# Two-stage SSD chunks and pinned gathered rows in a hybrid decoder layer

## The chip, the cores and the metric

The kernel runs on one core of one Trainium2 chip. The metric is device time in microseconds (us). The engines are named as the profile names them: PE is TensorE (matmul), PEld its weight load, DVE is VectorE, ACT is ScalarE, POOL is GpSimd and SP is SyncE, which only issues DMAs here.

## The reference

One decoder layer works on 16 meta tokens and 512 tokens of width 1024, in float32. Cut to what matters:

```python
u = rmsnorm(h, norm_mix_w)
z, xbc, dt_raw, conf_in = split(u @ w_in)
y_ssd  = ssd_mixer(z, xbc, dt_raw, ...)       # 16 heads in 4 groups, chunks of 128 tokens
y_conf = conformer_conv(conf_in, ...)         # GLU, depthwise conv of width 31, LayerNorm, silu
h = h + concat([y_ssd, y_conf]) @ w_out
h = h + peer_ffn(rmsnorm(h, norm_ffn_w), ...) # 8 heads x 16 of 128*128 single-neuron experts
out = rmsnorm(h, norm_final_w)[:, 16:]

# ssd, per group g and chunk c:
y  = (C B^T * exp(segsum(dt*a))) @ (dt*x) + exp(cumsum) * (C @ state)
state = state * exp(sum) + B^T @ (decay * dt * x)

# peer_ffn, per token: scores on two key halves, top 16 of each, top 16 of the sums, softmax gate
y = sum over the 128 chosen experts e of gelu(x . w_down[e]) * gate[e] * w_up[e]
```

## The kernel before, in words

The program is straight-line code. Tile, a scheduler at build time, orders the instructions of every engine by a priority, which is the order in which they are written, shifted by `early(n)` (as if written n instructions sooner) and `late(n)`, and by when a simulated timeline takes their inputs as ready. At run time each engine works through its own queue in that order and waits on semaphores.

*Mixer.* Nineteen weight blocks of the input projection are taken in the order of `ORDER`: `z` blocks (gate of the SSD), `x` blocks (x, B and C, with a convolution of width 4 and transposes through PE), and `c` blocks (conformer, with a convolution of 30 multiply-adds on DVE, L422, marked `late`). As soon as its inputs are there, `ssd(g)` is written for group g = 0 to 3, with `early(SSDP)`, so ahead of the convolutions. It goes through five chunks: chunk 0 holds the 16 meta tokens and makes only a state. Chunks 1 to 4 take PSUM tiles of one bank each: `pa` for B·C (L532) and C·state (L533), `pe` for the mask and the cumulated decay (L536, L539), from which ACT makes four exponentials (L545), and `pd` for the chunk's output product (L551) and its state product (L560). DVE multiplies the exponentials with B·C (L546), forms y from C·state (L548), the skip term (L549), the output product (L552) and the gate (L553), and carries the state on (L564, L565). The root mean square goes through ACT (L554) and POOL (L259), and y is stored to a DRAM buffer yD for groups 0 to 2. Tiles without a tag share four PSUM banks ("pb"): those of the SSD, of the transposes of the x blocks (L352, L355) and of the LayerNorm sums. The projections have four more ("pa").

*Output projection.* `out_part([0])` and `out_part([1])` use the SSD's half of the output, `out_part([2, 3])` the conformer's. Between them stand the LayerNorm sums (L657), the rows made of them on PE (L402) and the normalisation of eight blocks (L672 to L677). Weights are split into a high and a low part, the low one by an accumulating DMA from POOL's queue (L186).

*PEER.* Tokens 0 to 383 are computed densely over all experts: `down(i)` makes the activations of 128 experts, `up_prep(i)` and `up_mm(i)` gate them and multiply with w_up. Tokens 384 to 511 are computed sparsely: 128 rows of w_down and then of w_up, in four alternating batches of 32, are gathered by indirect DMAs (L895, on POOL), and DVE takes a dot product (L911) or an accumulation (L918) for each, 256 rows in all. `pump(x)` writes x of these rows, fractions carried over. The selection of experts (`second(t)`, for t = 3, 0, 1, 2) comes first. Then `gate_map` writes, for each of 12 blocks of 32 tokens, four quarters: one-hot maps on DVE (L946, L947, L949), products on PE (L954, L955) and copies on ACT (L957). 86 `down` blocks stand behind the gate maps in the text and are marked `early(AHP)`, so they are worked on at the same time. The main loop then goes over 128 expert blocks.

During the gate maps the gathered rows go through two buffers (`gat1`), in the main loop through six (`gat2`). `keep_in_program_order(r)` gives an instruction one added edge: in its engine's queue it stands behind the instruction that was written last before it on that engine. Gathers have it always, the row operations only when `paced` is filled, which before the change happens ahead of the main loop.

Of the kernel before, what the change touches and what calls it, by code (L numbers as in the profile page):

```python
# [15 lines left out]
AF = mybir.ActivationFunctionType  # L16
OP = mybir.AluOpType
# [18 lines left out]
LNP = 500  # L36
AHP = 1000
SPL = 0
SPRATE = (4.0, 1.03, 3.33, 0)
NQ = 2  # L40
NT = 4
HOLD = 2
# [75 lines left out]
def body(ctx, tc, I, out):  # L118
    nc = tc.nc
    V, S, G, E = nc.vector, nc.scalar, nc.gpsimd, nc.tensor  # L120
# [7 lines left out]
    def ps(tag="pb"):  # L128
        return psp.tile([128, 512], F32, name=tag, tag=tag)
# [4 lines left out]
    def late(n):  # L134
        return tc.high_priority(offset=-n)

    def mem(a, n):
        assert a + n <= SLAB
        return M[:, a:a + n]
# [13 lines left out]
    def load(dst, src):  # L153
        return nc.sync.dma_start(dst, src)
# [4 lines left out]
    def mm3(o, lh, ll, rh, rl, first, last):  # L159
        E.matmul(o, lh, rh, start=first, stop=False)  # L160
        E.matmul(o, lh, rl, start=False, stop=False)  # L161
        E.matmul(o, ll, rh, start=False, stop=last)  # L162
# [85 lines left out]
    def stat(n):  # L248
        a = stp[0] % 128
        if a + n > 128:  # L250
            a = 0
        stp[0] = a + n
        return st[:, a:a + n]

    def rstd_of(ss, n, scale, parts=128):
        v = stat(n)[:parts]
        V.tensor_scalar(v, ss, scale, EPS, op0=OP.mult, op1=OP.add)  # L257
        r = stat(n)[:parts]
        G.tensor_tensor(r, v, neghalf[:parts, :n], op=OP.pow)  # L259
        return r  # L260
# [31 lines left out]
    for n, t in enumerate(MO):  # L292
# [6 lines left out]
        r = rstd_of(ss, 1, 1.0 / D, parts)  # L299
        for half in range(2):  # L300
            hs = slice(512 * half, 512 * half + 512)
# [41 lines left out]
    Bt = mem(B0, 2048).rearrange("p (c n) -> p c n", c=4)  # L343
    BT = mem(BT0, 2112).rearrange("p (g t) -> p g t", g=4)
    CT = mem(CT0, 2048).rearrange("p (g t) -> p g t", g=4)
# [162 lines left out]
    h4 = lambda a: a.rearrange("p (h d) -> p h d", h=4)  # L508
    rot = [0]

    def ssd(g):
        dtv, nacs, eacs, cdB, wst, a3 = [DTV[k] for k in ("dtv", "nacs", "eacs", "cdB", "wst", "a3")]
        state = states[g % 2]
        ss = stat(4)
        ysl = []
        for c in range(5):
            np_ = NM if c == 0 else 128
            hs = slice(16 * c + 4 * g, 16 * c + 4 * g + 4)
            hb = lambda a: a[:np_, hs, None].to_broadcast([np_, 4, 64])
            n = rot[0]  # L520
            rot[0] += 1
            xc = XS[g % 2][:np_, c, :]
            xdt, xw = xdts[n % 3], xws[n % 3]
            V.tensor_tensor(h4(xdt[:np_]), h4(xc), hb(dtv), op=OP.mult)
            if c < 4:
                V.tensor_tensor(h4(xw[:np_]), h4(xdt[:np_]), hb(wst), op=OP.mult)
            pd = ps()
            if c > 0:
                t0 = 128 * (c - 1)
                V.tensor_tensor(h4(xc), h4(xc), rowb[:, 32 + 4 * g:36 + 4 * g, None].to_broadcast([128, 4, 64]), op=OP.mult)  # L530
                pa = ps()
                E.matmul(pa[:, 0:128], BT[:, g, NM + t0:NM + t0 + 128], CT[:, g, t0:t0 + 128], start=True, stop=True)  # L532
                E.matmul(pa[:, 128:384], CT[:, g, t0:t0 + 128], state, start=True, stop=True)  # L533
                pe = ps()
                pe4 = pe.rearrange("p (r l) -> p r l", r=4)
                E.matmul(pe4, identb, mnegb[:, None, :].to_broadcast([128, 4, 128]), start=True, stop=False)  # L536
                for r in range(4):
                    q = 16 * ((c - 1) % 2) + 4 * g + r
                    E.matmul(pe4[:, r, :], sel[:96, q:q + 1].to_broadcast([96, 128]),  # L539
                             a3[:96, 128 * ((c - 1) // 2):128 * ((c - 1) // 2) + 128],  # L540
                             start=False, stop=r == 3)
                em = EM[n % 3].rearrange("p (r l) -> p r l", r=4)
                for r in range(4):
                    h = 16 * c + 4 * g + r
                    S.activation(em[:, r, :], pe4[:, r, :], AF.Exp, bias=nacs[:, h:h + 1])  # L545
                V.tensor_tensor(em, em, pa[:, None, 0:128].to_broadcast([128, 4, 128]), op=OP.mult)  # L546
                y_ = ybs[n % 3] if g < 3 else YL[c - 1]
                V.tensor_tensor(h4(y_), h4(pa[:, 128:384]), hb(eacs), op=OP.mult)  # L548
                V.tensor_tensor(y_, y_, xc, op=OP.add)  # L549
                for r in range(4):  # L550
                    E.matmul(pd[:, 64 * r:64 * r + 64], em[:, r, :], xdt[:, 64 * r:64 * r + 64], start=True, stop=True)  # L551
                V.tensor_tensor(y_, y_, pd[:, 0:256], op=OP.add)  # L552
                V.scalar_tensor_tensor(y_, y_, 0.5, ZB[g % 2][:, c - 1, :], op0=OP.mult, op1=OP.mult)  # L553
                S.activation(xdt, y_, AF.Square, accum_out=ss[:, c - 1:c])  # L554
                rs = rstd_of(ss[:, c - 1:c], 1, 1.0 / 256)
                S.activation(y_, y_, AF.Copy, scale=rs)
                if g < 3:
                    load(yD[c - 1, :, 256 * g:256 * g + 256], y_)
            if c < 4:
                E.matmul(pd[:, 256:512], Bt[:np_, c, 128 * g:128 * g + 128], xw[:np_], start=True, stop=True)  # L560
                if c == 0:
                    S.activation(state, pd[:, 256:512], AF.Copy)
                else:
                    V.tensor_tensor(h4(state), h4(state), hb(cdB), op=OP.mult)  # L564
                    V.tensor_tensor(state, state, pd[:, 256:512], op=OP.add)  # L565


    done = set()
# [1 line left out]
    for o in ORDER:  # L570
        {"z": z_block, "x": x_block, "c": c_block}[o[0]](int(o[1]))
        if o == "z0":
            dt_chain()
        done.add(o)
        while left and {"x4", "x5", "x6", "x7", "x%d" % left[0], "z%d" % left[0]} <= done:
            with early(SSDP):
                ssd(left.pop(0))
# [104 lines left out]
    for t in range(4):  # L682
# [3 lines left out]
        for hf in range(2):  # L686
            hs = slice(512 * hf, 512 * hf + 512)
# [3 lines left out]
        r = rstd_of(ss, 1, 1.0 / D)  # L691
        for hf in range(2):
            hs = slice(512 * hf, 512 * hf + 512)
# [97 lines left out]
    for h in range(8):  # L791
        wh, wl = split_n(raw_n(I["wq"][h].rearrange("p c n -> p (c n)"), 2048), 2048, V)
        for f in range(2):
# [7 lines left out]
            for t in range(4):  # L801
                E.matmul(psc[:, 128 * t:128 * t + 128], qT[:, 128 * t:128 * t + 128], keys[:, 2 * h + f, :],
                         start=True, stop=True)
# [97 lines left out]
    paced = []  # L901
# [22 lines left out]
    def pump(x):  # L924
        spn[0] += x
        while spn[0] >= 1:
            spn[0] -= 1
            next(sp, None)

    for t in (3, 0, 1, 2):  # L930
        second(t)
        if t < 3:
            pump(SPRATE[3])

# [3 lines left out]
    def gate_map(n, b):  # L938
        gb = GBUF[n % 2]
        half = lambda a: a.rearrange("p t (j s) -> p t j s", s=2)  # L940
        io = iota16.rearrange("p (j s) -> p j s", s=2)[:, None].to_broadcast([128, TB, 64, 2])
        for q in range(GB // TB):
            t0 = GB * b + TB * q
            ob, oa = OB[q % 2], OA[q % 2]
            col = lambda a: a[:, t0:t0 + TB, None, :].to_broadcast([128, TB, 64, 2])
            V.tensor_tensor(half(ob), io, col(i2d), op=OP.is_equal)  # L946
            V.tensor_tensor(half(OE), io, col(i1d), op=OP.is_equal)  # L947
            for s in range(2):
                V.tensor_tensor(half(oa[s]), half(OE), col(gd[s]), op=OP.mult)  # L949
            for k0 in range(0, TB, 4):  # L950
                p = ps()
                for k in range(4):
                    po = p[:, 128 * k:128 * k + 128]
                    E.matmul(po, ob[:, k0 + k, :], oa[0][:, k0 + k, :], start=True, stop=False)  # L954
                    E.matmul(po, ob[:, k0 + k, :], oa[1][:, k0 + k, :], start=False, stop=True)  # L955
                c = TB * q + k0
                S.activation(gb.rearrange("p i t -> p t i")[:, c:c + 4, :], p.rearrange("p (t i) -> p t i", t=4),  # L957
                             AF.Copy, scale=1.0 / GS)
        for q in range(4 if n < NB - 2 else 0):
            load(GD[b, :, 32 * q:32 * q + 32, :], gb[:, 32 * q:32 * q + 32, :])  # L960

# [23 lines left out]
    def up_mm(i, Y, ops, ms, hfs=(0, 1)):  # L985
        sh, sl, wh, wl = ops
        f, l = i == 0, i == 127
        for m in ms:
            c = slice(128 * m, 128 * m + 128)
            for hf in hfs:  # L990
                d = slice(512 * hf, 512 * hf + 512)
                mm3(Y[m][hf], sh[:, c], sl[:, c], wh[:, d], wl[:, d], f, l)

    for n in range(NB):
        gate_map(n, n if n < NB - 2 else 2 * NB - 3 - n)
        with late(SPL):
            pump(SPRATE[0])

    with early(AHP):
        for i in range(NQ, NAHEAD):  # L1000
# [1 line left out]

    ring[0] = gat2
    gn[0] = 0
    paced.append(True)
    ops = {}
    Y = [[ps("pa"), ps("pa")], [ps("pa"), ps("pa")], [ps(), ps()]]
    for i in range(128):
        for j in {127 - NT: range(128 - NT, 128)}.get(i, () if i > 127 - NT else (i + 1,)):
            if NAHEAD <= j < 128:  # L1010
                down(j, "pb", False, V)
        pump(0 if i < HOLD else SPRATE[1] if i < NAHEAD else SPRATE[2])
        ops[i] = up_prep(i, V)
# [48 lines left out]
```

## Time and profile before

| | |
|---|---|
| median of 3 runs | 1705.93 us (1703.87 to 1708.15) |
| the profiled execution's own time | 1709.63 us |
| span in its profile | 1707.9 us |
| mean granted PE clock | 0.973 |
| DMA | 425.38 MB, mean 249 GB/s |

The span runs from the first to the last instruction; the time has some 2 us around it. The profile's page gives the busy time of each engine and, in 40 slices of 42.7 us, where it falls. Other views group instructions by line, list who waited for whom, list instructions in order of time, or sum up chosen stretches. In the timeline a row holds the start, the time, the engine, the line, the operation with output and inputs, and in brackets the idle time before it with what ended it. In a row of waits, "A <- B: 6.3, 4, 2.2" means that A waited for B 6.3 us in total, in 4 times, 2.2 us at the longest.

### The profile page before, as it was taken

What the parts mean: (1) busy time and instruction counts of PE and PEld (TensorE: products, weight loads), DVE (VectorE), ACT (ScalarE), POOL (GpSimd) and SP (SyncE); (2) the same over time, 40 slices, a digit from 0 to 9 for tenths busy, and PEclk for the clock granted to TensorE, in tenths of its full rate; (3) what the DMA queues carried; (4) which work ended last, traced back from release to release, by engine and by line L of the source; (5) the groups of instructions that cost most, each with busy time, mean ns of one, the idle gap of its engine ahead of it and who ended that gap; (6) DMA issues with size and microseconds to landing.
All of it is one profiled execution on the core that took longest, in us unless ns stands there. A gap on an engine that the chain in (4) does not pass through costs nothing. (4 is left out here: it accounts for less than half of the span.)

```text
span 1707.9 us, 26157 instructions
## 1 busy us (share of the span) xinstructions
PE 1643.6 (96%) x9529; PEld 1487.2 (87%) x9529; DVE 1397.6 (82%) x2864; ACT 770.7 (45%) x1155; POOL 397.6 (23%) x336
## 2 busy tenths in 40 slices
PE   7999999799899999899999999999999999999997
PEld 7999999577788999898889988888888899999996
DVE  4998999974469998989889458888888889888885
ACT  5566554445333344356668533333333333333333
POOL 1111110110000003233410013222222254454540
PEclk9999999589999999999999999999999999999999
DMA  6877574454422458799888679999999899999892
GB/s 209 194 176 164 143 163 123 141 136 119 128 83 75 131 177 271 271 301 327 306 308 301 211 233 364 347 348 357 352 341 355 317 341 363 357 347 348 324 328 86
DMA packets 165185, 425.38 MB, mean 249 GB/s; under 512 B 14384, under 2 KB 81200, under 8 KB 159424
## 3 DMA queue, kind: packets, MB, share of 16 engines
q1 hardware_dynamic: 121568, 261.17, 43.8%
q0 software_dynamic: 43488, 162.55, 31.4%
q8 instruction: 74, 1.21, 0.3%
q14 instruction: 55, 0.45, 0.1%
HBM read 381.72 MB, written 41.94 MB: 248 GB/s over the span
## 5 line engine op out<-in xcount | busy, mean ns | idle before, releaser
L161 PE MATMUL pa<-MR 128*128 128x512 f32 (+3 forms) x2120 | 731.3, 345 | 3.4 <-DMA MR<-wout 3.4
L160 PE MATMUL pa<-MR 128*128 128x512 f32 (+3 forms) x2120 | 728.5, 345 | 6.1 <-ACT M L777 1.7
L162 PE MATMUL pa<-MR 128*128 128x512 f32 (+3 forms) x2120 | 693.8, 345 | 6.5 <-DVE MR L755 5.1
L160 PEld LDWEIGHTS pa<-MR 128*128 128x128 f32 x2120 | 405.2, 191 | 38.6 <-ACT M L777 2.3
L162 PEld LDWEIGHTS pa<-MR 128*128 128x128 f32 x2120 | 404.0, 191 | 38.3 <-DVE MR L755 5.4
L161 PEld LDWEIGHTS pa<-MR 128*128 128x128 f32 x2120 | 404.9, 191 | 34.9 <-DMA MR<-wout 4.6
L754 ACT ACTIVATE MR<-M 128x1024 fp32r<-128x1024 f32 (+1 forms) x264 | 285.8, 1083 | 307.1 <-PE pa L161 130.4
L755 DVE TENSOR_TENSOR MR<-M,MR 128x1024 fp32r<-128x1024 f32 (+1 forms) x264 | 330.0, 1251 | 97.4 <-ACT MR L754 96.5
L895 POOL DMA_INDIRECT M<-wu,M x128 | 177.7, 1388 | 387.4 <-DVE M L918 255.6
L895 POOL DMA_INDIRECT M<-wd,M x128 | 156.2, 1220 | 471.8 <-DVE M L911 209.6
L161 PE MATMUL pb<-MR 128*128 128x384 f32 (+1 forms) x576 | 206.6, 359 | 0.0
L160 PE MATMUL pb<-MR 128*128 128x384 f32 (+1 forms) x576 | 206.6, 359 | 0.0
L162 PE MATMUL pb<-MR 128*128 128x384 f32 (+1 forms) x576 | 205.0, 359 | 0.0
L981 ACT ACTIVATE MR<-M 128x384 fp32r<-128x384 f32 x128 | 67.0, 523 | 262.2 <-issue 202.9
L918 DVE SCALAR_TENSOR_TENSOR M<-M 128x1024 f32<-128x1024 f32 x128 | 163.5, 1278 | 15.4 <-DMA M<-wu,M 15.1
L422 DVE SCALAR_TENSOR_TENSOR M<-M 128x512 f32<-128x512 f32 x240 | 173.6, 743 | 2.6 <-ACT M L420 1.5
L911 DVE SCALAR_TENSOR_TENSOR M<-M 128x1024 f32<-128x1024 f32 x128 | 154.6, 1218 | 14.0 <-DMA M<-wd,M 13.7
L160 PEld LDWEIGHTS pb<-MR 128*128 128x128 f32 x576 | 108.1, 188 | 11.3
L161 PEld LDWEIGHTS pb<-MR 128*128 128x128 f32 x576 | 108.1, 188 | 11.2
L982 DVE TENSOR_TENSOR MR<-M,MR 128x384 fp32r<-128x384 f32 x128 | 71.0, 555 | 56.6 <-ACT MR L981 56.6
L162 PEld LDWEIGHTS pb<-MR 128*128 128x128 f32 x576 | 108.1, 188 | 10.4
L957 ACT ACTIVATE M<-pb 128x512 f32<-128x512 f32 x96 | 97.3, 1151 | 36.8 <-PE pb L955 35.2
(221 smaller groups left out, 1485.4 us busy)
## 6 DMA issues: line engine op xcount, KB each, us to landing
M<-wdT SPq DMA_DIRECT2D x128, 512.0 KB, 5.1
M<-wu SPq DMA_DIRECT2D x128, 512.0 KB, 6.5
GD<-M SPq DMA_DIRECT2D x40, 512.0 KB, 6.3
M<-GD SPq DMA_DIRECT2D x32, 640.0 KB, 7.6
M<-win SPq DMA_DIRECT2D x19, 1024.0 KB, 5.5
MR<-win POOLq DMA_DIRECT2D x38, 512.0 KB, 6.7
HD<-M SPq DMA_DIRECT2D x88, 192.0 KB, 4.3
M<-HD SPq DMA_DIRECT2D x88, 192.0 KB, 6.2
```

Source lines behind the costliest of these rows:

```text
L160: E.matmul(o, lh, rh, start=first, stop=False)
L161: E.matmul(o, lh, rl, start=False, stop=False)
L162: E.matmul(o, ll, rh, start=False, stop=last)
L422: V.scalar_tensor_tensor(o, gl[:, j:j + 512], cw[:, j:j + 1], o, op0=OP.mult, op1=OP.add)
L754: S.activation(wh, raw, AF.Copy)
L755: leng.tensor_tensor(wl, raw, wh.bitcast(F32), op=OP.subtract)
L895: r = G.indirect_dma_start(out=g, out_offset=None, in_=src, in_offset=bass.IndirectOffsetOnAxis(ap=e3[:, k:k + 1], axis=0))
L911: use(V.scalar_tensor_tensor(g, g, 1.0, x2s, op0=OP.mult, op1=OP.mult, accum_out=dots[:, k:k + 1]))
L918: use(V.scalar_tensor_tensor(h1[3], g, act3[:, k:k + 1], h1[3], op0=OP.mult, op1=OP.add))
L957: S.activation(gb.rearrange("p i t -> p t i")[:, c:c + 4, :], p.rearrange("p (t i) -> p t i", t=4), AF.Copy, scale=1.0 / GS)
L981: S.activation(sh, sf, AF.Copy)
L982: V.tensor_tensor(sl, sf, sh.bitcast(F32), op=OP.subtract)
```

## The change

`ssd(g)` is written in two stages. `prepare(c)` holds all of a chunk that needs no state: the scaled inputs, B·C, the mask and the cumulated decay, the exponentials and their product with B·C. `finish(c)` holds C·state, the output and state products, the update of the state, and y. They are written as prepare(0), then for each c prepare(c+1) and finish(c). The output and state products go into the bank of the exponentials, so a chunk takes two banks instead of three; chunk 0 takes one for itself in `finish`. In `finish` the state is updated ahead of y.

The gathered rows are distributed anew. `SPRATE` holds, before and after: per gate map 4.0 (after all four quarters) and 3.0 (0.75 after each quarter); per main-loop block up to 87, 1.03 and 1.0; from 88 on, 3.33 and 3.3; after each of three selections 0 and 2; and, new, 6 after the last gate map. `paced` is filled ahead of the gate maps instead of ahead of the main loop, so each row operation there gets the added edge too.

```diff
-SPRATE = (4.0, 1.03, 3.33, 0)
+SPRATE = (3.0, 1.0, 3.3, 2, 6)
...
-        for c in range(5):
+        ready = {}
+
+        def heads(c, np_=128):
+            hs = slice(16 * c + 4 * g, 16 * c + 4 * g + 4)
+            return lambda a: a[:np_, hs, None].to_broadcast([np_, 4, 64])
+
+        def prepare(c):
             np_ = NM if c == 0 else 128
...
-            pd = ps()
+            em = pa = pe = None
             if c > 0:
...
                 pa = ps()
                 E.matmul(pa[:, 0:128], BT[:, g, NM + t0:NM + t0 + 128], CT[:, g, t0:t0 + 128], start=True, stop=True)
-                E.matmul(pa[:, 128:384], CT[:, g, t0:t0 + 128], state, start=True, stop=True)
                 pe = ps()
...
                 V.tensor_tensor(em, em, pa[:, None, 0:128].to_broadcast([128, 4, 128]), op=OP.mult)
+            ready[c] = n, np_, xc, xdt, xw, em, pa, pe
+
+        def finish(c):
+            n, np_, xc, xdt, xw, em, pa, pd = ready.pop(c)
+            hb = heads(c)
+            if c == 0:
+                pd = ps()
+            else:
+                t0 = 128 * (c - 1)
+                E.matmul(pa[:, 128:384], CT[:, g, t0:t0 + 128], state, start=True, stop=True)
+                for r in range(4):
+                    E.matmul(pd[:, 64 * r:64 * r + 64], em[:, r, :], xdt[:, 64 * r:64 * r + 64], start=True, stop=True)
+            if c < 4:
+                E.matmul(pd[:, 256:512], Bt[:np_, c, 128 * g:128 * g + 128], xw[:np_], start=True, stop=True)
+                if c == 0:
+                    S.activation(state, pd[:, 256:512], AF.Copy)
+                else:
+                    V.tensor_tensor(h4(state), h4(state), hb(cdB), op=OP.mult)
+                    V.tensor_tensor(state, state, pd[:, 256:512], op=OP.add)
+            if c > 0:
                 y_ = ybs[n % 3] if g < 3 else YL[c - 1]
...
+        prepare(0)
+        for c in range(5):
             if c < 4:
-                E.matmul(pd[:, 256:512], Bt[:np_, c, 128 * g:128 * g + 128], xw[:np_], start=True, stop=True)
...
+                prepare(c + 1)
+            finish(c)
...
+            pump(SPRATE[0] / 4)
...
+    paced.append(True)
     for n in range(NB):
         gate_map(n, n if n < NB - 2 else 2 * NB - 3 - n)
-        with late(SPL):
-            pump(SPRATE[0])
+    pump(SPRATE[4])
...
-    paced.append(True)
```

More of the change, by code (lines that the diff above doesn't have):

```diff
@@ L514, in ssd @@
         ss = stat(4)
-        ysl = []
-        for c in range(5):
+        ready = {}
[3 more added lines that the diff above has]
+        def prepare(c):
             np_ = NM if c == 0 else 128
-            hs = slice(16 * c + 4 * g, 16 * c + 4 * g + 4)
-            hb = lambda a: a[:np_, hs, None].to_broadcast([np_, 4, 64])
+            hb = heads(c, np_)
             n = rot[0]
@@ L549, in ssd @@
                 V.tensor_tensor(y_, y_, xc, op=OP.add)
-                for r in range(4):
-                    E.matmul(pd[:, 64 * r:64 * r + 64], em[:, r, :], xdt[:, 64 * r:64 * r + 64], start=True, stop=True)
                 V.tensor_tensor(y_, y_, pd[:, 0:256], op=OP.add)
@@ L558, in ssd @@
                     load(yD[c - 1, :, 256 * g:256 * g + 256], y_)
+        prepare(0)
+        for c in range(5):
             if c < 4:
-                E.matmul(pd[:, 256:512], Bt[:np_, c, 128 * g:128 * g + 128], xw[:np_], start=True, stop=True)
[L561 to L565, printed above, removed]
+                prepare(c + 1)
+            finish(c)
     done = set()
```

## The prediction

> **What bounds the kernel now.** I read the page of the profile first, then the table of stretches, then the waits of each engine in the two places where TensorE is not full, then the timeline there. The page says that TensorE (PE) is the engine to feed, and where it starves.
>
> ```profile
> span 1707.9 us, 26157 instructions
> PE 1643.6 (96%) x9529; PEld 1487.2 (87%) x9529; DVE 1397.6 (82%) x2864; ACT 770.7 (45%) x1155; POOL 397.6 (23%) x336
> ...
> PE   7999999799899999899999999999999999999997
> ...
> DVE  4998999974469998989889458888888889888885
> ...
> PEclk9999999589999999999999999999999999999999
> ```
>
> A slice is 42.7 us. PE has a hole in slice 8 (from 299 us), with a granted clock near half, and small ones in slices 11 and 17; VectorE (DVE) is full at the first hole. The next table puts stretches side by side; its columns are length, then PE, weight load, DVE, ACT and POOL busy time, granted clock, share of the DMA engines and GB/s.
>
> ```profile
> 300.00:340.00 40.00, 28.27 (x99) 20.83 (x100) 39.85 (x89) 16.80 (x47) 5.56 (x5) 0.53 0.49 147
> 360.00:386.60 26.60, 23.74 (x114) 20.02 (x113) 12.96 (x40) 13.29 (x31) 3.01 (x4) 0.74 0.45 119
> 386.60:408.00 21.40, 18.91 (x87) 15.21 (x85) 18.77 (x31) 15.77 (x20) 0.91 (x1) 0.98 0.41 99
> 680.00:700.00 20.00, 14.57 (x72) 13.93 (x71) 20.00 (x67) 3.85 (x6) 3.50 (x4) 0.83 0.67 218
> 820.00:840.00 20.00, 17.48 (x127) 16.06 (x127) 14.63 (x20) 9.89 (x12) 7.51 (x3) 0.91 0.90 311
> 950.00:1018.00 68.00, 66.60 (x378) 63.95 (x377) 24.41 (x30) 26.88 (x38) 5.07 (x5) 1.00 0.69 225
> 1020.00:1680.00 660.00, 660.00 (x3128) 573.97 (x3127) 560.57 (x835) 240.22 (x329) 244.49 (x201) 1.00 0.94 340
> ...
> 600.00:1018.00 418.00, 401.66 (x2754) 385.65 (x2753) 341.73 (x680) 226.93 (x286) 90.02 (x56) 0.99 0.79 271
> ```
>
> From 1020 to 1680 us PE is busy in all 660 us at full clock: whatever the change does to DVE, POOL or the gathers there is hidden behind PE, unless a row comes so late that the loop waits. Two stretches can give time. In the mixer (300 to 408 us) DVE is full until 340 (39.85 of 40) and PE waits for it. In the gate maps PE is idle for 418 - 401.66 = 16.3 us between 600 and 1018, and DVE has 68 - 24.41 = 43.6 us of slack only after 950, when the maps are done and PE works off queued down products alone.
>
> **The change, part by part: the SSD.** It adds and removes no arithmetic: the same DVE, ACT and PE instructions and the same store to yD per chunk are issued in another order. What moves: the next chunk's xdt, xw, B·C product, mask, exponentials and decay product stand ahead of this chunk's state work, and the C·state product leaves the first stage. The waits inside SSD that this addresses:
>
> ```profile
> DVE M L552 <- PE pb L551: 3.6, 6, 0.7
> DVE M L546 <- PE pb L533: 3.4, 5, 2.0
> ...
> PE pb L551 <- DVE M L546: 6.3, 4, 2.2
> PE pb L533 <- DVE M L565: 2.7, 2, 1.4
> ```
>
> The first two rows (40 to 360 us) are DVE standing still, 7.0 us, because the decay product (L546) reads a bank into which the state product (L533) is still to be written, and because y (L552) waits for products issued just before. The last two (300 to 378 us) are PE standing in its queue for DVE; DVE is full there, so on the path they count only as far as DVE gets work sooner. DVE bounds this stretch, so the gain can't be PE's whole loss; it is what DVE idles, and what its order delays. This is the order now, first on DVE, then on PE:
>
> ```profile
> 360.02 0.69 DVE L424 TENSOR_TENSOR M<-M 128x512 f32<-128x512 f32 x1
> ...
> 368.33 0.68 DVE L546 TENSOR_TENSOR M<-M,pb 128x512 f32<-128x512 f32 x1
> ...
> 377.41 0.17 DVE L659 TENSOR_SCALAR M<-pb 128x8 f32<-128x8 f32 x1 [4.92 <-PE pb L657]
> ...
> 379.51 0.17 DVE L667 TENSOR_TENSOR M<-M 128x4 f32<-128x4 f32 x1
> ...
> 386.66 4.87 DVE L672 TENSOR_TENSOR M<-M,pb 128x512 f32<-128x512 f32 x8 [2.50 <-PE pb L402]
> ...
> 392.65 3.07 DVE L673 TENSOR_TENSOR M<-M,pb 128x512 f32<-128x512 f32 x5
> ...
> 404.97 3.09 DVE L677 TENSOR_TENSOR MR<-M,MR 128x512 fp32r<-128x512 f32 x5
> ```
>
> ```profile
> 369.15 1.49 PE L551 MATMUL pb<-M 128*128 128x64 f32 x8 [1.15 <-DVE M L546]
> 370.44 6.93 PE L657 MATMUL pb<-M 128*128 128x1 f32 x32
> ...
> 385.57 1.95 PE L402 MATMUL pb<-M 128*128 128x128 f32 x16
> ...
> 408.44 0.80 PE L161 MATMUL pa<-MR 128*128 128x512 f32 x1 [2.83 <-DMA MR<-wout]
> ```
>
> The last convolution ends at 360.7 us. The last SSD chunk is only then at its decay product (368.3), the LayerNorm sums (L657) stand behind that chunk in PE's queue, and LayerNorm is applied from 386.66 to 408.06. PE starts the output projection's conformer half in earnest at 408.44. My steps:
>
> 1. Of the 7.0 us of DVE waits I take 5; chunk 1 of each group still has nothing ahead of it. Bounds 0 and 7.0.
> 2. Between 360 and 386.6 DVE idles 26.6 - 12.96 = 13.6 us. If the SSD is done before the convolution, its DVE work stands before 360 instead of after, which is neutral, and what must remain is the chain of sums: 6.93 (L657) + 1.95 (L402) + 379.68 - 377.41 = 2.3 for the small operations from L659 to L667 = 11.2. Gain 13.6 - 11.2 = 2.4. With the half clock of L657 gone too it would be 2.4 + 3.5 = 5.9, without any effect 0.
> 3. LayerNorm then starts at 386.66 - 5 - 2.4 = 379.3. PE needs its first four k slices: 4.87 (eight L672), eight L673 at 3.07/5 = 0.61, 4.9 and four L677 at 3.09/5 = 0.62, 12.3 us in all, hence 391.6 against 408.44: 16.8 us. Now this stretch is longer because additions of the first half of the projection stand between, and because the weights' low halves land late (the 2.83 us wait).
>
> I take 12 of the 16.8: the weights' low halves must land earlier too, and the first half of the projection has to be finished by 391 (it runs until 404 now). Bounds 0 and 16.8 + 3.5 = 20.3; a loss of up to 5 stands for an order in which the exponentials issued ahead delay another block.
>
> The clock has a say in step 2. In the first row of the stretches it is 0.53 over 40 us although PE is busy 28.27 of 40 and its longest wait named above is 2.2 us. The Trainium skill (TensorE: Matmul & The Clock Gate, Part 1) says that the clock halves after an idle window of about 3.4 us. By that rule gaps of 2.2 us would not have cost the clock here; the measured row disagrees, and it decides. By the rule L657 would run at full clock after the change, and the SSD term would be 12 + 3.5 = 15.5 us; by the row I leave it at 12.
>
> New waits: the chunk's output product now goes into the bank of the exponentials, so it waits for four ACT reads, which are issued a chunk earlier; ACT is busy 16.80 of 40 us, so this lies beside other work. If ACT were late, PE would stand at the chunk's state product and behind it the projections; this is the first rival. A slot of xdt is rewritten two chunks after its square is taken instead of three, which the same half-idle ACT covers; uncovered it would cost DVE one square per chunk.
>
> **The gate maps.** No row is added: 48 rows are processed before the main loop as before, now 2 after three of the four selections (6), 0.75 after each of 48 quarters (36) and 6 at the end; the 42 latter stand behind the last DVE instruction traced before them. Now they float, and this is what it costs:
>
> ```profile
> DVE M L918 <- DMA M<-wu,M: 15.1, 6, 5.3
> DVE M L911 <- DMA M<-wd,M: 13.7, 12, 2.8
> ...
> PE pb L954 <- DVE M L949: 8.3, 8, 2.5
> ...
> PE pa L162 <- DVE MR L755: 5.1, 1, 5.1
> ```
>
> DVE stands 28.8 us for gathered rows, and behind it are the one-hot products (L949) for which PE waits 8.3 us. The reason lies in these rows, of the line views of the gather, the row product and the one-hot product:
>
> ```profile
> L895 POOL DMA_INDIRECT M<-wd,M x32: 936/1346/2362, 637.0 to 772.6; - x32
> DMA to landing us min/median/max: 4.3/6.7/11.5
> ...
> L911 DVE SCALAR_TENSOR_TENSOR M<-M x32: 1203/1217/1227, 642.4 to 781.1; 128x1024 f32<-128x1024 f32 x32
> ...
> L949 DVE TENSOR_TENSOR M<-M x96: 668/683/693, 681.7 to 949.2; 128x1024 f16<-128x1024 f16 x96
> ```
>
> The gathers go through two buffers. One round is 1.35 (POOL) + 6.7 (landing) + 1.22 (row) = 9.3 us, 4.6 us a row; the rows run at (781.1 - 642.4)/31 = 4.5 us. They run as fast as the ring turns, and every slow landing holds DVE. A quarter of a map takes (949.2 - 681.7)/48 = 5.6 us, so 0.75 row a quarter is a row every 7.4 us and 14.9 us a round, against 9.3 (14.1 with the slowest landing). DVE waits then almost vanish, except in the bursts of 6. The last 6 lie in the slack after 950.
>
> Worth on PE: 8.3 us of waits, and the clock lost behind them, (1 - 0.91) x 20 = 1.8 us in 820 to 840, together 10.1. I take 9, leaving 1.1 for waits in the bursts. Upper bound: add 5.1 us before L162 and 0.17 x 20 = 3.4 us of clock in 680 to 700, 18.6; there DVE is full with the selections and early rows, of which fewer will be there. Lower bound 0. Moved past: POOL's queue carries in this stage only gathers, SP's stores of the map (GD) stay behind their quarter, and the rows carry no transfer of their own beside the gather.
>
> **The main loop.** 1.0 row instead of 1.03 up to block 87 and 3.3 instead of 3.33 after it: 256 - 48 - 86 = 122 rows at 3.3 end at block 125 of 127, one later than now ((256 - 48 - 88.6)/3.33 = 35.9, block 124). The cover is PE's 660 of 660 us; the tail keeps four blocks of prepared work after the last row. Cost 0.
>
> **The sum**, against the profiled execution's own 1709.63 us: 1709.6 - 12 - 9 = 1688.6. That execution is 3.7 us above the median of the runs shown (1705.93), so in their terms 1705.9 - 21 = 1685.
>
> **The rivals.** *Only the gate maps gain.* The two-bank chunk turns the look-ahead into PE waits: with four banks of this tag, chunk c+1 takes the two free ones and the transposes of the x blocks, which need the same tag, wait as before; SSD and convolution then end where they do. For it speaks that DVE, not PE, is full until 340. 1705.9 - 9 = 1697. The Trainium skill (PSUM — Partial Sum Buffer, PSUM bank collisions raise a hardware error) says to guard by bank, not address; the L546 row above, waiting for a product in other columns of its bank, agrees.
>
> *Only the SSD gains*: PE's waits for L949 come from the DVE load itself (341.73 of 418 us) and remain. Against it: the waits lie in the stretches with the longest stalls (820 to 840: DVE only 14.63 of 20). 1705.9 - 12 = 1694.
>
> *Both at their upper bounds*: 1705.9 - 20.3 - 18.6 = 1667.
>
> *Nothing arrives*: the reordered queues lose elsewhere what they gain; 1701 to 1711.
>
> *Slower*: pinned rows stand before their data. If each of 42 rows meets a gather issued only one quarter earlier, it waits 1.35 + 6.7 - 5.6 = 2.45 us, 103 us in all. 28.8 us of that is there already and 43.6 us is slack after 950, so 30 us come on top: 1705.9 - 12 + 30 = 1724. It decides from 28.8 + 43.6 = 72.4 us of row waits, 1.7 us a row. Against it: two buffers give two quarters.
>
> **How the numbers follow.** The forecast (both gain, 1677 to 1693) gets 0.44, gate maps alone 0.14, SSD alone 0.12, both at the bounds 0.10, nothing 0.10, slower 0.10. A measurement of this kernel tells about 0.3% (5 us) from no change. So faster 0.80, the same 0.10, slower 0.10. The range 1666 to 1706 leaves out the slower case, the upper half of "nothing", and little below.
>
> **What would show it.** In the changed profile: the row of L546 waiting for L533 gone; the last SSD chunk before the last convolution's L424; the first LayerNorm product near 379 us and PE dense from about 392 us; DVE waits for gathered rows under 10 us between 600 and 1018, PE's waits for L949 near 1; the main loop starting about 21 us earlier and as long as before. It would be wrong if the last SSD chunk still followed the convolution, if LayerNorm started no earlier, or if DVE's waits for rows grew.

## The result, and the profile after

The changed kernel takes 1675.45 us (median of 4 runs, 1674.39 to 1679.32) against 1706.58 us of the kernel before in the same session: a ratio of 0.9823, with a 95% interval of 0.9803 to 0.9844, so 31 us. The forecast was 1685 with a range of 1666 to 1706. The direction and the range held. The time lies 1.5 us below the 1677 to 1693 us of the outcome that was forecast: one term of the sum was far too small and one too large, and that the two errors partly cancel is luck.

From the page of the changed kernel:

```profile
span 1673.3 us, 26114 instructions
PE 1623.7 (97%) x9529; PEld 1471.4 (88%) x9529; DVE 1395.8 (83%) x2864; ACT 769.8 (46%) x1155; POOL 396.2 (24%) x336
...
PE   7999999888899999999999999999999999999997
...
DVE  5999899994478999999998478888888888888876
...
PEclk9999999789999999999999999999999999999999
```

No engine does less: DVE's busy time is 1395.8 against 1397.6 us. PE's falls by 20 us, as the mean granted clock rises from 0.973 to 0.986. The hole in slice 8 is shallower and the one in slice 17 is gone. Busy times by stretch, with the columns of the table in the prediction:

```profile
300.00:340.00 40.00, 33.52 (x144) 26.65 (x143) 38.72 (x84) 16.11 (x40) 5.54 (x6) 0.81 0.48 134
340.00:360.00 20.00, 12.33 (x48) 8.98 (x47) 19.74 (x43) 9.28 (x21) 1.88 (x2) 0.74 0.62 144
360.00:400.00 40.00, 33.26 (x160) 28.04 (x159) 29.40 (x52) 20.00 (x23) 2.81 (x3) 0.91 0.46 119
...
600.00:980.00 380.00, 378.34 (x2655) 364.06 (x2654) 324.27 (x603) 216.85 (x273) 86.30 (x55) 1.00 0.84 290
980.00:1640.00 660.00, 660.00 (x3122) 572.97 (x3121) 560.02 (x834) 239.66 (x326) 242.69 (x201) 1.00 0.96 342
```

Between the queries and the main loop PE idles 380 - 378.34 = 1.7 us instead of 16.3, at full clock. The main loop is as full as before. In the mixer, PE has a new hole at 340 to 360 us, where DVE is still full.

A landmark in each stage shows where the profiled executions part: the first transpose behind the mixer, then the first gated block of the main loop. Of the kernel before, in two views by line:

```profile
L591 PE MATMUL pb<-M x32: 270/273/447, 454.9 to 468.7; 128*128 128x128 f32 x32
```

```profile
L981 ACT ACTIVATE MR<-M x128: 506/525/528, 991.9 to 1684.1; 128x384 fp32r<-128x384 f32 x128
```

And of the kernel after (L611 and L1002 are the same instructions):

```profile
L611 PE MATMUL pb<-M x32: 270/273/445, 439.2 to 454.0; 128*128 128x128 f32 x32
```

```profile
L1002 ACT ACTIVATE MR<-M x128: 506/525/528, 958.5 to 1649.6; 128x384 fp32r<-128x384 f32 x128
```

The mixer ends 454.9 - 439.2 = 15.7 us earlier, and the main loop begins 991.9 - 958.5 = 33.4 us earlier: 17.7 us come from PEER ahead of the loop. The loop and the tail make up the last 1.2 us of the 34.6 us between the two spans. Single executions mislead on the first number, as the experiments show.

### The profile page after: what moved, and what is told of

The parts are those of the page before. It is cut to its first block, busy times and chain, and to the rows that moved or that the text cites. A ratio compares the mean times of both kernels' runs of the same rounds, so it can differ in the third digit from the quotient of the medians.

```text
span 1673.3 us, 26114 instructions
## 1 busy us (share of the span) xinstructions
PE 1623.7 (97%) x9529; PEld 1471.4 (88%) x9529; DVE 1395.8 (83%) x2864; ACT 769.8 (46%) x1155; POOL 396.2 (24%) x336
## 5 line engine op out<-in xcount | busy, mean ns | idle before, releaser
L775 DVE TENSOR_TENSOR MR<-M,MR 128x1024 fp32r<-128x1024 f32 (+1 forms) x264 | 330.4, 1253 | 81.9 <-ACT MR L774 80.7
L915 POOL DMA_INDIRECT M<-wd,M x128 | 160.0, 1250 | 548.1 <-DVE M L931 283.7
L915 POOL DMA_INDIRECT M<-wu,M x128 | 169.0, 1320 | 307.9 <-DVE M L938 263.4
L1002 ACT ACTIVATE MR<-M 128x384 fp32r<-128x384 f32 x128 | 67.0, 523 | 274.1 <-issue 203.5
L161 PEld LDWEIGHTS pb<-MR 128*128 128x128 f32 x576 | 108.1, 188 | 11.3
L977 ACT ACTIVATE M<-pb 128x512 f32<-128x512 f32 x96 | 99.0, 1159 | 37.4 <-PE pb L975 33.4
```

Source lines behind the costliest of these rows:

```text
L775: leng.tensor_tensor(wl, raw, wh.bitcast(F32), op=OP.subtract)
L915: r = G.indirect_dma_start(out=g, out_offset=None, in_=src, in_offset=bass.IndirectOffsetOnAxis(ap=e3[:, k:k + 1], axis=0))
L1002: S.activation(sh, sf, AF.Copy)
```

## The experiments

### The two parts by themselves

```diff
# e1: the kernel before, with ssd(g) of the kernel after
# e2: the kernel after, with ssd(g) of the kernel before
```

> The kernel before with the two-stage SSD alone; rows distributed and queued as before. In the two traces the transposes ahead of PEER (L591 before, L611 after) start 15.7 us earlier and the rest of the 34.6 us comes later. Theory A (the two parts are independent): the mixer's 15 us and nothing else, 1706.6 - 15 = 1692, with PE still waiting about 8 us for the one-hot products. Rival B (the gate maps gained because the mixer handed over in another order): 1680 or less. Rival C (the mixer's gain needs the other part): above 1700.

Measured: 1698.2 us, ratio 0.9950 (0.9931 to 0.9970).

> The kernel after with the SSD of before; only the rows' distribution and their place in the queue are new. Theory A (independent parts): the gate maps' 19 us, 1706.6 - 19 = 1688, PE idle under 3 us between the end of the queries and the main loop. Rival B (needs the mixer's new order): above 1697.

Measured: 1681.8 us, ratio 0.9848 (0.9823 to 0.9873).

The parts are independent (8.0 + 24.4 = 32.4 us apart against 31 together), but not as the profiles had it: the SSD is worth 8.0 us alone and 1681.8 - 1675.5 = 6.4 us on top of the rows, and the rows 24.4 and 1698.2 - 1675.5 = 22.7 us. In e2 every engine's queue is the same as before until the expert selection. Still its mixer ended sooner than that of the profiled execution before. By line, in e2:

```profile
L591 PE MATMUL pb<-M x32: 270/273/446, 450.5 to 464.3; 128*128 128x128 f32 x32
```

450.5 against 454.9 us for the same order: the profiled execution of before was one of the slower ones (1709.6 against a median of 1706 to 1707). Some 4 us of the 15.7 are no effect of the change. Against e2 the kernel after ends its mixer 11.3 us sooner, which is still more than the 6.4 us of the medians; e2's own profiled execution (1685.4 us) is 3.6 us above its median.

### The rows: the edge, the distribution, the waits

```diff
# e3: the edge is given only ahead of the main loop
-    paced.append(True)
     for n in range(NB):
...
     gn[0] = 0
+    paced.append(True)
# e4: the edge stays; four rows after each map
-SPRATE = (3.0, 1.0, 3.3, 2, 6)
+SPRATE = (4.0, 1.0, 3.3, 0, 0)
...
-            pump(SPRATE[0] / 4)
...
         gate_map(n, n if n < NB - 2 else 2 * NB - 3 - n)
+        pump(SPRATE[0])
```

> The kernel after, but row operations get the added edge only ahead of the main loop, as before; the new distribution stays. Theory P (the edge makes the gain: without it rows float to where the ring turns as fast as it can): DVE's waits for rows within the maps go back from 11 to some 28 us, PE waits about 8 us for one-hot products, time 1675.5 + 10 = 1685. Rival S (the distribution alone makes it): 1675 to 1678, waits unchanged.

Measured: 1699.0 us, ratio 0.9948 (0.9926 to 0.9969).

> The kernel after with the edge kept, but the old distribution: four rows at once after each map, none after the selections, none at the end. Theory S (spacing matters, the ring turns once in 9.3 us for two rows): of each four rows two find no buffer filled, 2 x (4.6 - 1.25) = 6.7 us of DVE waits a map, 80 us in all against 43.6 us of slack, so PE waits again, 1690 to 1715. Rival P (the edge alone makes the gain): 1675 to 1680.

Measured: 1682.1 us, ratio 0.9859 (0.9820 to 0.9897).

With e1 this makes a table of four, all with the new SSD. (In e4 the main loop keeps the new 1.0 and 3.3 rows a block; only the rows ahead of it are distributed as before.) Without the edge the distribution is worth nothing (1698.2 old, 1699.0 new). With the edge the old distribution has 1682.1 and the new one 1675.5. So the edge alone brings 16 us. The 6.6 us of the spacing on top are not clear of the noise: the four runs of e4 lie between 1678.3 and 1689.3 us, those of the kernel after between 1674.4 and 1679.3. Who waited in e3, PE and DVE, from the end of the queries on:

```profile
PE pb L974 <- DVE M L969: 11.1, 7, 2.2
PE pa L162 <- DVE MR L775: 5.4, 1, 5.4
...
DVE M L938 <- DMA M<-wu,M: 16.2, 5, 5.5
...
DVE M L931 <- DMA M<-wd,M: 14.1, 13, 2.6
```

Both waits of PE in the kernel before are back: for the one-hot products (L969) and, once, 5.4 us for a weight split (L775). In the kernel after, the same view has:

```profile
DVE M L938 <- DMA M<-wu,M: 14.5, 9, 3.6
DVE M L931 <- DMA M<-wd,M: 9.0, 8, 3.0
...
PE pa L160 <- ACT M L797: 1.4, 1, 1.4
```

DVE still waits 23.5 us for rows, and PE only 0.3 us for DVE, and for no one-hot product. The sum is therefore not what counts. By stretches of time, the wait for accumulated rows in the kernel after, from 640 to 900 and from 900 to 980 us:

```profile
DVE M L938 <- DMA M<-wu,M: 2.6, 3, 1.7
...
DVE M L938 <- DMA M<-wu,M: 11.9, 6, 3.6
```

The last one-hot product starts at 907 us. From 640 to 900 us, within the maps, DVE waits 2.6 + 8.4 (dot products) = 11.0 us instead of the 28.8 before, at most 3.0 us at once, and PE waits for none of it. Another 11.9 us fall behind the last one-hot product, where PE has queued products and is busy in all 46 us from 912 to 958. In e4 the waits from 560 us to 900 are 9.1 us, and 18.7 us come later. The edge moves half of the waits or more to the last maps and behind them rather than removing them: the last of the 48 rows starts at 863 us in e3 and at 933 us in the kernel after.

Are the waits the cause, or the rows' own DVE time in front of the maps? The next kernel leaves the edge out and lets the first 48 rows read a resident buffer.

```diff
-                g = gather(I["wd"], k)
+                g = row(I["wd"], k)     # the first 48: one resident buffer, no gather
...
-                g = gather(I["wu"], k)
+                g = row(I["wu"], k)
```

> The kernel without the added edge in the gate maps (1699.0), in which the 48 rows ahead of the main loop are not gathered: they read one resident buffer that is filled from the expert indices, so DVE does the same row work and can't wait for a DMA; the gathers and their transfers of these rows are left out. Theory W (DVE's waits for landings, 30 us, are what PE's waits come from): PE's waits for one-hot products under 2 us, 1680 or less. Rival Q (the rows' own DVE time, 60 us placed ahead of the maps and the weight splits, is what costs): PE's waits stay near 10 us, 1692 to 1700.

Measured: 1685.4 us, ratio 0.9877 (0.9856 to 0.9899). PE's waits from 560 to 1010 us:

```profile
PE pa L162 <- DVE MR L775: 3.0, 1, 3.0
PE pa L160 <- ACT M L797: 1.8, 2, 1.4
PE pa L160 <- ACT MR L774: 0.9, 1, 0.9
```

PE waits no more for one-hot products, and the way from the mixer's end to the main loop is 963.2 - 441.8 = 521.4 us, against 540.2 in e3 (442.1 to 982.3) and 519.3 in the kernel after. So 18.8 of e3's 20.9 us hang on the gathers and the waits for their landings; row work without them costs some 2 us against the kernel after. The 48 transfers are left out too, so a part could be their traffic; that was not tried apart. The main loop and the tail of e9 took longer (963.2 to 1671.5 from the first gated block to the first final addition, 708.3 us against 697.4), hence a time above the 1680 expected. In that loop DVE waits 51.6 us for dot-product rows, in 24 times, where the kernel after has no wait for them above 1 us; why they land late there was not tried.

The other side of the ring is twice the rate.

```diff
-SPRATE = (3.0, 1.0, 3.3, 2, 6)
+SPRATE = (6.0, 0.8, 2.9, 2, 6)
```

> The kernel after with 1.5 pinned rows a quarter instead of 0.75 (84 ahead of the main loop instead of 48; the main loop takes 0.8 and 2.9 a block). One row then falls on 3.7 us, and two buffers turn at 4.6 us a row. Theory ring: DVE waits 72 x 0.9 = 65 us for landings and does 36 rows x 1.25 = 45 us more, so the maps end about 100 us later than at 907; the slack behind them (50 us) is gone and the main loop starts some 50 us later, 1725. Rival (the edge alone keeps PE fed, because weight splits pass the rows): 1675 to 1685.

Measured: 1704.1 us, ratio 0.9995 (0.9975 to 1.0016). The stretch around the maps' end and DVE's waits from 560 to 1000 us:

```profile
900.00:1010.00 110.00, 93.03 (x546) 85.92 (x545) 70.88 (x87) 42.94 (x56) 37.51 (x23) 0.94 0.82 276
```

```profile
DVE M L938 <- DMA M<-wu,M: 36.7, 17, 4.9
DVE M L931 <- DMA M<-wd,M: 15.6, 9, 2.8
```

At a row on 3.7 us DVE waits 52.3 us, against the 65 worked out, and PE idles 17 us from 900 to 1010 us, 11.0 of them for the first blocks of the main loop. The price is 29 us and not 50. The maps end at 935 us, 28 us later and not 100: rows pile up behind the maps and run into the main loop, which starts at 979 us, 20.5 us later than in the kernel after, and is 17 us longer. This profiled execution took 1712.4 us, 8 us above the median, and the rates of the main loop were lowered too, so how much of the longer loop is the ring's is open. The rival, that the edge alone is enough, falls: at this rate the whole gain is lost.

### The SSD: which of its moves

```diff
# e5: no look-ahead
-        prepare(0)
         for c in range(5):
-            if c < 4:
-                prepare(c + 1)
+            prepare(c)
             finish(c)
# e6: a bank of its own for output and state products
-            if c == 0:
-                pd = ps()
-            else:
+            pd = ps()
+            if c > 0:
# e7: state product and update behind y again, in finish
-            if c < 4:
-                E.matmul(pd[:, 256:512], Bt[:np_, c, 128 * g:128 * g + 128], xw[:np_], start=True, stop=True)
...
             if c > 0:
                 y_ = ybs[n % 3] if g < 3 else YL[c - 1]
...
+            if c < 4:
+                E.matmul(pd[:, 256:512], Bt[:np_, c, 128 * g:128 * g + 128], xw[:np_], start=True, stop=True)
...
# e11: ssd(g) of before; output product, state product and update ahead of y
                 V.tensor_tensor(em, em, pa[:, None, 0:128].to_broadcast([128, 4, 128]), op=OP.mult)
+                for r in range(4):
+                    E.matmul(pd[:, 64 * r:64 * r + 64], em[:, r, :], xdt[:, 64 * r:64 * r + 64], start=True, stop=True)
+            if c < 4:
+                E.matmul(pd[:, 256:512], Bt[:np_, c, 128 * g:128 * g + 128], xw[:np_], start=True, stop=True)
...
+            if c > 0:
                 y_ = ybs[n % 3] if g < 3 else YL[c - 1]
# e12: e5 and e6 together
```

> The kernel after, written as prepare(c), finish(c) for each chunk: two banks and the state updated ahead of y, but the next chunk is not issued ahead. The SSD's share is 6 to 8 us so far (1681.8 without it against 1675.5, 1706.2 against 1698.2). Theory A (the look-ahead makes it): back to 1681 or more. Rival B (the early state update and the smaller number of banks make it, since a scheduler with free banks can reorder by itself): 1675 to 1677.

Measured: 1676.9 us, ratio 0.9824 (0.9800 to 0.9848).

> The kernel after with a bank of its own for the output and state products again, taken in finish; look-ahead and order stay. Theory A (look-ahead needs the two-bank chunk, as four banks then hold two chunks): 1679 to 1682, the last SSD chunk later than 330 us. Rival B (the exponentials' bank is free by then anyway, the sharing is worth nothing): 1675 to 1677.

Measured: 1673.3 us, ratio 0.9802 (0.9779 to 0.9826), the fastest kernel of this study; its interval overlaps that of the kernel after, so the two aren't told apart.

> The kernel after with the state product and the state's update behind y again, as before the change; look-ahead and two banks stay. Theory A (look-ahead makes the gain): 1675 to 1677. Rival B (the early state update shortens the chain from chunk to chunk): 1679 to 1682.

Measured: 1682.5 us, ratio 0.9858 (0.9834 to 0.9882).

> The SSD of before (three banks a chunk, nothing issued ahead) with one thing moved: output and state products and the state's update stand ahead of y. Rows as in the kernel after. The last runs gave 1681.8 with the old SSD, 1676.9 without look-ahead, 1673.3 with a bank of its own, 1682.5 with the state last. Theory A (the early state update is the whole of the SSD's gain): 1673 to 1677, the last decay product near 330 us instead of 365. Rival B (it takes two of the three parts): 1679 to 1682.

Measured: 1681.2 us, ratio 0.9861 (0.9842 to 0.9880).

> The kernel after with a bank of its own for output and state products and without look-ahead: what is left of the SSD's change is that C·state stands behind the decay product and the state's update ahead of y. C·state late with the state last gave 1682.5, the state first with C·state early 1681.2, both with look-ahead and own bank 1673.3, both without look-ahead in two banks 1676.9. Theory A (the two moves together are the gain, look-ahead adds nothing): 1673 to 1677. Rival B (without sharing, look-ahead is needed, as the scheduler otherwise takes chunks one by one): 1680 or more.

Measured: 1676.2 us, ratio 0.9816 (0.9789 to 0.9842).

The look-ahead itself is worth 1.4 us with two banks and 3.0 with three, which these runs can't tell from nothing; sharing the bank shows no gain either. Two other moves make the gain, and neither does it alone: the state's update ahead of y (without it 1682.5, about the 1681.8 of the old SSD) and the C·state product behind the decay product (without it, in e11, 1681.2; this was the part that its expectation did not name). One thing is left open: e11 takes its bank for the output and state products at the chunk's start, e12 only behind the decay product, so the place of the C·state product and the moment of taking that bank are not told apart. And each of these edits lets the scheduler order the other instructions anew, so the runs show what an order is worth and not a single dependency. The view by line of the decay product, whose last entry is the last chunk's start, says the same. In order, e2 (old SSD), e11, e7, e12 and e6:

```profile
L546 DVE TENSOR_TENSOR M<-M,pb x16: 668/684/689, 157.9 to 364.9; 128x512 f32<-128x512 f32 x16
```

```profile
L546 DVE TENSOR_TENSOR M<-M,pb x16: 672/687/689, 158.0 to 349.4; 128x512 f32<-128x512 f32 x16
```

```profile
L549 DVE TENSOR_TENSOR M<-M,pb x16: 668/677/681, 148.0 to 353.7; 128x512 f32<-128x512 f32 x16
```

```profile
L549 DVE TENSOR_TENSOR M<-M,pb x16: 667/678/687, 155.2 to 337.9; 128x512 f32<-128x512 f32 x16
```

```profile
L549 DVE TENSOR_TENSOR M<-M,pb x16: 668/678/689, 148.3 to 314.9; 128x512 f32<-128x512 f32 x16
```

One move brings the last chunk from 365 to between 349 and 354 us and leaves the time where it was; both bring it to 338 or sooner, and the time falls. In e11 PE then stands in its queue for DVE and ACT, in the view of PE's waits from 240 to 460 us:

```profile
PE pa L601 <- ACT M L564: 7.9, 2, 6.7
PE pa L160 <- ACT MR L677: 7.2, 1, 7.2
PE pb L550 <- DVE M L526: 6.0, 1, 6.0
```

The kernel after has a wait like the second (6.7 us, shown below), but none like the other two, of which the first is for the last steps of y (L564 on ACT).

### LayerNorm's sums ahead of the projection

```diff
-        out_part([1])
+        out_part([1], (0,))
...
         prs = to_rows(rst)
         prh = to_rows(rho)
+    with early(YP), tc.issue_after(tr_last[0].ins):
+        out_part([1], (1,))
```

> The kernel after with the second half of out_part([1]) written behind the LayerNorm sums and their rows (L402) and queued behind them on PE. In the profile after, PE puts 21 matmuls (4.8 us) between the two parts of the sums and 21 more (4 us) ahead of L402, while DVE idles 8 us between 372 and 384 us. If DVE's way to LayerNorm bounds the mixer: LayerNorm from about 379 instead of 384, time 1670 to 1673. If PE's work bounds it (the matmuls only change places): 1675 to 1677, and if PE idles ahead of the sums: 1680.

Measured: 1678.2 us, ratio 0.9832 (0.9809 to 0.9856). LayerNorm starts at 380.4 instead of 384.2 us, but the transposes behind the mixer at 440.5 instead of 439.2: the matmuls put behind the sums are missed ahead of them. PE now idles 2.1 us ahead of the sums, for the last convolution, and 2.2 us ahead of the rows made of them, where the kernel after idles at neither. This is nearer to the third outcome than to the first.

## Why the prediction was right, and where it was not

**Step 1 (5 of 7.0 us of DVE waits in the SSD): failed.** The two rows are gone, but two of the same size stand in their place, 7.1 us (L533, which the prediction calls the state product, is the C·state product): the state's update now waits for the C·state product that still reads the state, and y for the same product. In the kernel after, from 40 to 360 us:

```profile
DVE M L567 <- PE pb L559: 5.2, 4, 1.7
...
DVE M L571 <- PE pb L559: 1.9, 2, 1.6
```

**Steps 2 and 3 (LayerNorm at 379.3, PE dense from 391.6): the end was right, the way was not.** In time order, on DVE:

```profile
329.63 0.69 DVE L549 TENSOR_TENSOR M<-M,pb 128x512 f32<-128x512 f32 x1
...
371.73 0.69 DVE L424 TENSOR_TENSOR M<-M 128x512 f32<-128x512 f32 x1
...
384.15 4.87 DVE L692 TENSOR_TENSOR M<-M,pb 128x512 f32<-128x512 f32 x8 [0.20 <-PE pb L402]
388.94 4.87 DVE L693 TENSOR_TENSOR M<-M,pb 128x512 f32<-128x512 f32 x8
```

and on PE:

```profile
370.40 1.84 PE L677 MATMUL pb<-M 128*128 128x1 f32 x16
...
376.96 1.84 PE L677 MATMUL pb<-M 128*128 128x1 f32 x16
...
383.06 1.95 PE L402 MATMUL pb<-M 128*128 128x128 f32 x16
...
391.75 0.80 PE L160 MATMUL pa<-MR 128*128 128x512 f32 x1 [6.74 <-ACT MR L696]
```

The last SSD chunk does come before the last convolution (329.6 against 371.7), as foretold. But SSD work and additions now stand ahead of the convolution on a full DVE, which ends at 372.4 instead of 360.7; and the sums are parted by projection matmuls. LayerNorm starts only 2.5 us earlier, and 4 us later than e2's 380.0, which has the old SSD; beside e2, the sign that LayerNorm starts no earlier came true. What moved is the first half of the projection: PE ends it at 383 instead of 404, so nothing stands between the normalised blocks, and PE starts on the first high part. That 391.6 was met at 391.75 is luck: LayerNorm started 4.9 us later than worked out, and PE stood 7.6 us behind that start instead of 12.3. The start of this second half of the projection goes with the time in all orders tried: 401.6 us in e2, 398.0 in e11 and 401.9 in e7, but 393.4 in e5, 392.2 in e12 and 391.3 in e6. That the new SSD gains because it lets PE catch up while DVE convolves is read from these traces; no run tries it by itself.

**The SSD term, 12 us: mis-sized, 6.4 to 8.0.** It was worked out on one execution whose mixer was some 4 us late, and the way of steps 1 to 3 was not the one that gained.

**The gate-map term, 9 us: mis-sized, 22.7 to 24.4.** The rival with both terms at their upper bounds had 18.6 for it, which by the medians was still low. In the traces the way from the mixer's end to the main loop is 17.7 us shorter than before (519.3 against 537.0) and 20.9 us shorter than in e3, near that bound; the rest lies within what executions of one kernel differ by. I took PE's waits for one-hot products and the clock of one slice. The hole at 680 to 700 us (5.1 us and the clock behind it), which I left out, had the same cause: floating rows; e3 brings it back with 5.4 us, and of these e9, whose rows float but wait for no landing, keeps 3.0. The sentence that DVE's waits would almost vanish was wrong: 28.8 became 23.5 us, of which 11.0 lie within the maps; the forecast was under 10 in all.

**The slower rival.** Its mechanism exists: in e8 rows wait until the slack behind the maps is gone. Its point was set at 72.4 us of waits; in e8, 52.3 us together with 36 more rows and a longer main loop were enough to lose 29 of the 31 us.

**The clock.** The half-clock rule of the Trainium skill (TensorE: Matmul & The Clock Gate, Part 1) was set against a stretch at 0.53 with waits of at most 2.2 us (2.3 with one for a DMA that was not named). After the change PE is busy 33.5 instead of 28.3 of the 40 us from 300, and the clock there is 0.81. The LayerNorm sums run at full speed, 16 in 1.84 us against 32 in 6.93, which is the outcome that I gave to the rule and not the one I kept: PE is busy without a gap from 356 us until they start. The kernel after has a case that agrees with the rule, too: after its one wait of 6.7 us the granted clock is 0.50 from 391.8 to 397.0 us.

**The main loop at no cost: right.** From the first gated block to the first final addition it takes 697.4 instead of 698.5 us.

## What to carry to other kernels

Where an engine works in order, ask where in its queue a wait for a transfer stands, not how long all such waits are: 23.5 us of them, half behind the last urgent instruction and the rest spread out, cost PE nothing, and 30 us of them in front of it cost some 19. One added edge that keeps early-ready work from floating forward was worth more than the pipelining beside it. Before a gain is put down to a restructured loop, take its moves apart: here two small ones, effective only together in these runs, made it, and the look-ahead was not needed.

## What was not expected of the hardware

The PE clock can be at half without any long gap: in the kernel before it is 0.50 from 310 to 330 us, where PE is busy 13.5 of 20 us and never waits more than 2.3 us at once. Which measure of activity counts, these runs do not separate. And one order of instructions does not end the mixer at one time: before and e2 end it 4.4 us apart (454.9 and 450.5 us), and the kernel after, e1, e3, e4 and e8, whose engines run the same instructions in the same order until 637 us, between 439.0 and 442.1 us. A difference of a few us in this stage needs medians.
